# Fused decoder block on one core: output projection split along its contraction, fixed homes for the mixer's tiles, and engine orders from the layer's timeline machine

## The chip, the cores and the metric

The kernel runs as one launch on one core of a Trainium2 chip. A core has five engines that run side by side, each through its own list of instructions in the order in which they stand there: TensorE (PE in the profile, with its weight loads as PEld), VectorE (DVE), ScalarE (ACT), GpSimd (POOL) and SyncE (SP), which here does nothing but issue DMA transfers. The metric is the time of the core in microseconds of device time, lower is better: the median of several runs.

## What is computed

One decoder block over 512 tokens with 2048 channels, in float32. The heart of the reference:

```python
sh1, sc1, gt1, sh2, sc2, gt2 = jnp.split(mod[:, None, :], N_MOD, axis=-1)   # mod = silu(c) @ w_ada + b_ada
h = _rmsnorm(x, norm1_g[l]) * (1.0 + sc1) + sh1
p = h @ w_in[l]
y_rwkv = _rwkv7_mixer(p[..., :N_RWKV_COLS], ...)
y_pool = _pool_mixer(p[..., N_RWKV_COLS:], ...)
mix = jnp.concatenate([y_rwkv, y_pool], axis=-1) @ w_out[l]
x = x + gt1 * mix
h = _rmsnorm(x, norm2_g[l]) * (1.0 + sc2) + sh2
x = x + gt2 * _conv_ffn(h, w_up[l], conv_w[l], conv_b[l], w_down[l])
```

The RWKV mixer has 16 heads of 64 channels, with a state of 64 x 64 per head that is carried from token to token. The pool mixer takes the causal mean over windows of 2, 4, 8 and 16 tokens, for 256 channels each, and multiplies it by a 256 x 256 matrix.

## The kernel before

Everything lies transposed: channels on the 128 partitions, the 512 tokens along them. So x is 16 tiles of 128 x 512. A float32 product is made of three products of the shorter float32r (`mm3`, L115 to L117): the weights are split into a high part `whi` (a copy on ScalarE, L109) and the rest `wlo` (a subtraction on VectorE, L111), the activations likewise (`ah`, `al`). `project` does that for one output tile: it loads weights in pieces of 128 x 512 (`wraw`, ring of 4) and runs 3 products of 128 x 512 for each 128 rows of the contraction. Such a product is called a full-width product below.

The stages in order:

1. The first third of the adaLN product (`ada1`), the first norm, and the first 8 of 35 tiles of the input projection, which are accumulated in all PSUM banks at once.
2. The mixers. The RWKV heads are worked off in four *quads* of four heads (`quad`, g = 0 to 3), two column tiles each. A quad first makes its decays and keys (L376 to L418), then the scores inside chunks of 64 tokens (L427), turns tiles over (L439), inverts 64 x 64 triangular matrices (16 x 16 blocks on VectorE, L478 to L487, then two *levels* of products, L504 to L521), and then goes through the 8 chunks one after the other. This last part is called *the chain* here: for each chunk, state to right-hand side (L538, L540 on VectorE), times the inverse (L544, copied by ScalarE in L545), new state (L554, L557, then L562 on VectorE). After it come the output, its norm and its gate (L571 to L606), and the result is stored to DRAM in `mixd`. All these are small products (64 x 64 and the like), and each step waits for the one before it on another engine.
   Beside the quads run the remaining tiles of the input projection (`win_tile`, 48 full-width products each): the tiles for the next quad in `win_pair` (six for each quad, shifted by a token and stored in DRAM until they are needed), and after the last quad the eight tiles of the pool mixer, each pool group's sums (L274) and products (L289) following its two tiles.
   Beside the quads run also 192 pieces of the adaLN product (`ada_rest`, 48 for each quad): a 128 x 512 piece of weights is loaded (`war`, ring of 3, 256 KB) and multiplied and summed on VectorE (L341).
3. The output projection: 8 output tiles are accumulated at once in blocks of four contraction tiles (`out_block`), then two tiles in full, then the last six in two halves of 256 tokens (`out_half`), so that the second norm of one half runs beside the other.
4. The gated feed-forward part, with the last 64 pieces of the adaLN product in its first group, the second residual and the last norm.

What sets the order: the kernel is written as one sequence with Tile; a scheduler then gives each engine its list. The quads stand under `tc.high_priority(offset=100000)`, so the scheduler takes their instructions first whenever it believes that they can run, and fills in with the rest. The tiles of a quad come from one ring of 12 buffers (`quad_tile`, tag `q4`), in the order of their allocation. All DMA transfers are issued by SP in one list.

Of the kernel before, what the change touches and what calls it, by code (L numbers as in the profile page):

```python
# [46 lines left out]

WIN_ORDER = ["T0", "T1", "T2", "r0", "k0", "v0", "r1", "k1", "v1"]
for _p in range(2, NP):
    WIN_ORDER += [f"r{_p}", f"k{_p}", f"v{_p}"]  # L50
WIN_ORDER += [f"u{_j}" for _j in (6, 7, 2, 3, 4, 5, 0, 1)]


MIX_ORDER = [14, 15, 10, 11, 12, 13, 0, 1, 2, 3, 4, 5, 6, 7, 8, 9]
# [3 lines left out]
def block_kernel(ctx, tc, a, out, stop=None, dbg=None):  # L58
# [16 lines left out]
    scanm = cp.tile([P, 2 * NK, C + 1], F32, tag="scanm", name="scanm")  # L75
    nc.gpsimd.memset(scanm, 1.0)
    nc.gpsimd.memset(scanm[:, :, 0:1], 0.0)
    lanei = cp.tile([P, 16, 16], F32, tag="lanei", name="lanei")
    nc.sync.dma_start(lanei, a["lanei"][:, :, :])
# [25 lines left out]
    def split_weights(src, eng=V):  # L105
        raw = wp.tile([P, WC], F32, tag="wraw", name="wraw", bufs=4)
        nc.sync.dma_start(raw, src)
        hi = wp.tile([P, WC], F32R, tag="whi", name="whi", bufs=3)
        S.copy(hi, raw)  # L109
        lo = wp.tile([P, WC], F32R, tag="wlo", name="wlo", bufs=3)  # L110
        eng.tensor_tensor(lo, raw, hi[:, :].bitcast(F32), op=ALU.subtract)  # L111
        return hi, lo
# [6 lines left out]
    def project(ps, src, acts, start=True, stop=True, engs=(V,)):  # L119

        n = len(acts)
        for k0 in range(0, n, WC // P):
            wh, wl = split_weights(src[:, k0 * P : k0 * P + WC], engs[k0 // 4 % len(engs)])
            for kk in range(WC // P):
# [47 lines left out]
    if True:  # L172
# [53 lines left out]
        if True:  # L226
# [5 lines left out]
            def quad_tile(name):  # L232
                return ra.tile([P, 2 * (16 + T)], F32, tag="q4", name=name, bufs=12)
# [7 lines left out]
            xg = two(quad_tile("xg"))  # L241
# [13 lines left out]
            rkv0 = [quad_tile(n) for n in "rkv"]  # L255
# [4 lines left out]
    def load_pw(gi):  # L260
        t = ra.tile([P, T], F32, tag="war", name="pw", bufs=3)
        pw = t.rearrange("p (i d) -> p i d", i=2)
# [3 lines left out]
    def padded(name):  # L266
        return quad_tile(name).rearrange("p (x t) -> p x t", x=2)

    def pool_front(gi, upad):
        win = WINS[gi]  # L270
        cur, lo, step = upad, 1, 1
        while step < win:
            nxt = padded("sw")
# [4 lines left out]
        z = two(quad_tile("z"))  # L278
        V.scalar_tensor_tensor(z, cur[:, :, 16:], 1.0 / win, upad[:, :, 16:], op0=ALU.mult, op1=ALU.subtract)
        V.tensor_mul(z[:, :, 0:win], cur[:, :, 16 : 16 + win], prec[:, None, 0:win].to_broadcast([P, 2, win]))  # L280
        V.tensor_sub(z[:, :, 0:win], z[:, :, 0:win], upad[:, :, 16 : 16 + win])
        return z

    def pool_back(gi, z, pw):
        ps = batch()
        mx = two(quad_tile("mxp"))
        for d in range(2):
            for i in range(2):
                PE.matmul(ps[:, d, :], pw[:, i, d * P : (d + 1) * P], z[:, i, :], start=i == 0, stop=i == 1)  # L289
            j = gi * 2 + d  # L290
            S.activation(mx[:, d, :], ps[:, d, :], AF.Identity, bias=drv[:, 35 + j : 36 + j], scale=col("psc", j))
            if gi:
                nc.sync.dma_start(mixd[8 + j], mx[:, d, :])
            else:
                last_mix.append(split_act(14 + d, mx[:, d, :]))
# [19 lines left out]
    HEADS = [(x, h) for h in range(2) for x in range(2)]  # L315

# [8 lines left out]
    dx = tc.dram_tile([2, 2, C, 2 * NK, C], F32, name="dx")  # L325
    for w in range(2):
        nc.sync.dma_start(dx[w].rearrange("s i j t -> (s i) (j t)"), sall[:, :, :, :].rearrange("p x c t -> p (x c t)"))

    cq = [None]
    modq = ra.tile([P, 4, 48], F32, tag="modq", name="modq")  # L330

    def ada_rest(n0, n1):
        for n in range(n0, n1):
            kq, j = divmod(n, 48)
            if j == 0:
                cq[0] = ra.tile([P, T], F32, tag="cq", name="cq")
                nc.sync.dma_start(cq[0], cact[0:1, kq * T : (kq + 1) * T].partition_broadcast(P))
            wa = ra.tile([P, T], F32, tag="war", name="war", bufs=3)
            nc.sync.dma_start(wa, a["ada2"][kq, j, :, :])
            jk = ra.tile([P, T], BF16, tag="jkr", name="jkr")  # L340
            V.scalar_tensor_tensor(jk, wa, 1.0, cq[0], op0=ALU.mult, op1=ALU.mult,  # L341
# [20 lines left out]
    def quad(g, rkv):  # L362
# [15 lines left out]
        sg = quad_tile("sg")  # L378
        V.memset(lead(sg)[:, :, 0:1], 0.0)
# [3 lines left out]
        al = quad_tile("al")  # L383
        for x in range(2):
            S.activation(two(al)[:, x, :], psal[:, x, :], AF.Sigmoid, bias=c2("a0", x))
        cs = quad_tile("cs")
        n = 2 * NK * (C + 1)
        V.tensor_tensor_scan(cs[:, 0:n], scanm[:, :, :].rearrange("p c t -> p (c t)"), sg[:, 0:n], 0.0,
                             op0=ALU.mult, op1=ALU.add)
        mid = ra.tile([P, 2 * NK, 1], F32, tag="mid", name="mid")  # L390
        V.tensor_copy(mid, lead(cs)[:, :, C // 2 : C // 2 + 1])
        V.tensor_sub(lead(cs), lead(cs), mid[:, :, :].to_broadcast([P, 2 * NK, C + 1]))
        ep = quad_tile("ep")
        S.activation(ep[:, 0:n], cs[:, 0:n], AF.Exp, scale=-Q)
        em = quad_tile("em")
        S.activation(em[:, 0:n], cs[:, 0:n], AF.Exp, scale=Q)
        fdec = ra.tile([P, 2 * NK - 1, 1], F32, tag="fdec", name="fdec")
# [588 lines left out]
```

## Time and profile before

| | |
|---|---|
| median of 3 runs | 2460.82 us (2457.5 to 2462.72) |
| the profiled execution, its own time | 2459.58 us |
| its span from the first to the last instruction | 2457.8 us |
| TensorE busy | 2254.7 us (92%), 14178 instructions |
| VectorE busy | 1345.9 us (55%) |
| ScalarE busy | 831.7 us (34%) |
| moved by DMA | 352.98 MB, 144 GB/s on average |
| granted TensorE clock, mean | 0.970 |

How to read it: the span is cut into stages by what TensorE does in them. In the part from 1400 us to 2400 us TensorE has work in every microsecond; there, only fewer or shorter products could change the time. Before 722 us it waits in many places, and there the time hangs on which waits end last. "Idle before, releaser" in a row of the trace is how long the engine stood still before that instruction and what ended it. PEclk is the share of full clock that TensorE was granted.

### The profile page before, as it was taken

The numbers are of one execution on the slowest core, as the hardware profiler recorded it, in microseconds if no ns is written. First come the engines' busy times: TensorE is split into PE (matmuls) and PEld (weight loads), VectorE is DVE, ScalarE is ACT, GpSimd is POOL, SyncE is SP. The second block draws the span as 40 slices with busy tenths as digits, with TensorE's granted clock in tenths as the row PEclk, the third lists the DMA queues.
The fourth block names the chain that finished last, engine by engine and source line by source line (L and its number), as shares of the span: only waits on it lengthen the run. The fifth ranks groups of instructions, "written<-read, shape, count | busy, mean of one in ns | idle before, by whom it ended". The sixth has DMA issues, their size and how long they took to land.

```text
span 2457.8 us, 36667 instructions
## 1 busy us (share of the span) xinstructions
PE 2254.7 (92%) x14178; PEld 1829.3 (74%) x14178; DVE 1345.9 (55%) x2398; ACT 831.7 (34%) x1351; POOL 23.5 (1%) x26
## 2 busy tenths in 40 slices
PE   4878888888379999999999999999999999999997
PEld 3656566565257889987888888888888888888887
DVE  7987686766434457757634443444344434444457
ACT  3243252523233335532223322333233322323333
POOL 0000000000000001100000000000000000000000
PEclk9989899999679999999999999999999999999998
DMA  9965757656103635538532233333323332332335
GB/s 357 340 221 163 240 176 222 213 177 208 40 32 120 198 111 181 190 105 260 170 98 98 95 98 96 99 96 97 97 97 99 95 99 95 98 97 97 99 97 174
DMA packets 204418, 352.98 MB, mean 144 GB/s; under 512 B 46033, under 2 KB 52049, under 8 KB 200017
## 3 DMA queue, kind: packets, MB, share of 16 engines
q1 hardware_dynamic: 204242, 350.63, 44.7%
q8 instruction: 111, 1.82, 0.3%
q14 instruction: 65, 0.53, 0.1%
HBM read 335.33 MB, written 15.21 MB: 143 GB/s over the span
## 4 chain that ended last, share of the span: by engine, by line
PE 63%; DMA 2%; DVE 2%; ACT 0%; issue 0%; POOL 0%; DVEq 0%; SPq 0%; ACTq 0%; POOLq 0%
PE b L115 20%; PE b L117 19%; PE b L116 19%; DMA slot<-ada 1%; DMA wraw<-wup 1%; PE bt L115 1%; PE bt L117 1%; PE bt L116 1%; DVE slot L810 1%; PE mm L115 0%; PE mm L117 0%; PE mm L116 0%; DVE wlo L111 0%; PE bt L289 0%; DVE x L863 0%
## 5 line engine op out<-in xcount | busy, mean ns | idle before, releaser
L111 DVE TENSOR_TENSOR wlo<-wraw,whi 128x512 fp32r<-128x512 f32 x772 | 532.3, 692 | 714.9 <-ACT whi L109 700.4
L109 ACT CAST whi<-wraw 128x512 fp32r<-128x512 f32 x788 | 488.5, 622 | 1240.7 <-PE b L116 931.2
L117 PE MATMUL b<-hh,wlo 128*128 128x512 f32 (+1 forms) x1472 | 560.6, 381 | 7.1 <-DVE wlo L111 6.8
L115 PE MATMUL b<-hh,whi 128*128 128x512 f32 (+1 forms) x1472 | 559.9, 380 | 0.0
L116 PE MATMUL b<-hl,whi 128*128 128x512 f32 (+1 forms) x1472 | 559.5, 380 | 0.0
L115 PE MATMUL b<-ah,whi 128*128 128x512 f32 (+1 forms) x992 | 353.3, 357 | 1.9 <-ACT whi L109 1.9
L117 PE MATMUL b<-ah,wlo 128*128 128x512 f32 (+1 forms) x992 | 352.1, 355 | 0.8 <-DVE wlo L111 0.8
L116 PE MATMUL b<-al,whi 128*128 128x512 f32 (+1 forms) x992 | 352.2, 355 | 0.0
L117 PEld LDWEIGHTS b<-hh,wlo 128*128 128x128 f32 x1472 | 277.0, 188 | 62.8 <-DVE wlo L111 9.5
L116 PEld LDWEIGHTS b<-hl,whi 128*128 128x128 f32 x1472 | 277.0, 188 | 52.5
L115 PEld LDWEIGHTS b<-hh,whi 128*128 128x128 f32 x1472 | 277.0, 188 | 52.4 <-ACT whi L109 0.6
L115 PEld LDWEIGHTS b<-ah,whi 128*128 128x128 f32 x992 | 187.7, 189 | 30.9 <-ACT ah L136 2.3
L117 PEld LDWEIGHTS b<-ah,wlo 128*128 128x128 f32 x992 | 187.7, 189 | 27.3 <-DVE wlo L111 1.2
L116 PEld LDWEIGHTS b<-al,whi 128*128 128x128 f32 x992 | 187.7, 189 | 27.2 <-DVE al L137 1.2
L117 PE MATMUL mm<-ah,wlo 128*128 128x512 f32 x464 | 190.4, 410 | 14.7 <-DVE wlo L111 14.7
L115 PE MATMUL mm<-ah,whi 128*128 128x512 f32 x464 | 189.3, 408 | 8.7 <-ACT whi L109 8.7
L116 PE MATMUL mm<-al,whi 128*128 128x512 f32 x464 | 187.7, 404 | 0.0
L341 DVE SCALAR_TENSOR_TENSOR jkr<-war,cq 128x512 bf16<-128x512 f32 x192 | 132.1, 688 | 60.9 <-DMA war<-ada 50.5
L117 PEld LDWEIGHTS mm<-ah,wlo 128*128 128x128 f32 x464 | 88.4, 191 | 43.8 <-DVE wlo L111 22.3
L848 DVE SCALAR_TENSOR_TENSOR x<-b,mod,x 128x512 f32<-128x512 f32 x80 | 59.7, 750 | 110.9 <-PE b L117 110.8
L115 PEld LDWEIGHTS mm<-ah,whi 128*128 128x128 f32 x464 | 88.7, 191 | 32.5 <-ACT whi L109 9.1
L116 PEld LDWEIGHTS mm<-al,whi 128*128 128x128 f32 x464 | 88.5, 191 | 21.7 <-issue 3.5
(267 smaller groups left out, 1926.4 us busy)
## 6 DMA issues: line engine op xcount, KB each, us to landing
wraw<-wup SPq DMA_DIRECT2D x368, 256.0 KB
war<-ada SPq DMA_DIRECT2D x192, 256.0 KB
wraw<-wdn SPq DMA_DIRECT2D x192, 256.0 KB
wraw<-win SPq DMA_DIRECT2D x140, 256.0 KB
wa<-ada SPq DMA_DIRECT2D x32, 1024.0 KB
wraw<-wout SPq DMA_DIRECT2D x88, 256.0 KB
slot<-ada SPq DMA_DIRECT2D x64, 256.0 KB
sp<-spill SPq DMA_DIRECT2D x18, 256.0 KB
```

Source lines behind the costliest of these rows:

```text
L109: S.copy(hi, raw)
L111: eng.tensor_tensor(lo, raw, hi[:, :].bitcast(F32), op=ALU.subtract)
L115: PE.matmul(ps, wh, xh, start=start, stop=False)
L116: PE.matmul(ps, wh, xl, start=False, stop=False)
L117: return PE.matmul(ps, wl, xh, start=False, stop=stop)
L341: V.scalar_tensor_tensor(jk, wa, 1.0, cq[0], op0=ALU.mult, op1=ALU.mult, accum_out=modq[:, kq, j : j + 1])
L810: V.scalar_tensor_tensor(jk, wa, 1.0, cbs[kq], op0=ALU.mult, op1=ALU.mult, accum_out=modg[:, kq, j : j + 1])
L848: V.scalar_tensor_tensor(x2[f], ps, mod[:, 80 + f : 81 + f], x2[f], op0=ALU.mult, op1=ALU.add)
```

## The change

- **Order.** `TileContext(nc, schedule_with_timeline_sim=True)`: the engines' lists now come from the layer's timeline machine.
- **Input projection.** The tiles of the pool groups are made before the tiles of the last quad, in the iteration g = 2; they are stored to DRAM (`su`) and loaded again by `pool`. The four pool groups stand behind the third quad, under high priority, and their results go to `mixd` all four.
- **Output projection.** The contraction is ordered as pool tiles, then quads 0 to 3. For the first `NW` = 10 output tiles the first `NM` = 14 of 16 contraction tiles are done while the last quad runs: product, times the gate, plus x, stored as `part` in DRAM. The last quad's result is split at once into `M[14:16]` and never goes to DRAM. Afterwards `part` comes back as x2 and only the two last contraction tiles are added. The tiles 10 to 15 are done in halves as before.
- **adaLN product.** The same 96 x 2048 numbers are cut into 96 pieces of 128 x 1024 (512 KB), 24 for each quad; the ring `war` has 2 buffers, which the pool matrices `pw` share; the product is written over its input instead of to a bfloat16 tile.
- **Quads.** `quad` is split into `front` and `rest`. Each tile has a home of its own (`cell(tag)`: R, K, V, X, Y, EM, EP, AL, INV, TB, TK, TV, PM) instead of a place in a ring. The inverse's transpose Y is made by TensorE and ScalarE from X (L536, L539) instead of through DRAM; X is cleared by GpSimd and only its diagonal blocks are loaded (8 transfers after one store, for 24 stores and 2 loads). One preloaded table set serves Ln and Exp. In the chain, the two products of the new state change places.

The core of the diff:

```diff
-MIX_ORDER = [14, 15, 10, 11, 12, 13, 0, 1, 2, 3, 4, 5, 6, 7, 8, 9]
+MIX_ORDER = [8 + 2 * _g + _i for _g in POOLS for _i in range(2)] + [0, 1, 2, 3, 4, 5, 6, 7]
+NM = 14
...
     def load_pw(gi):
-        t = ra.tile([P, T], F32, tag="war", name="pw", bufs=3)
+        t = ra.tile([P, 2 * T], F32, tag="war", name="pw", bufs=2)
...
-            wa = ra.tile([P, T], F32, tag="war", name="war", bufs=3)
+            wa = ra.tile([P, 2 * T], F32, tag="war", name="war", bufs=2)
             nc.sync.dma_start(wa, a["ada2"][kq, j, :, :])
-            jk = ra.tile([P, T], BF16, tag="jkr", name="jkr")
-            V.scalar_tensor_tensor(jk, wa, 1.0, cq[0], op0=ALU.mult, op1=ALU.mult,
+            V.scalar_tensor_tensor(wa, wa, 1.0, cq[0], op0=ALU.mult, op1=ALU.mult,
                                    accum_out=modq[:, kq, j : j + 1])
...
+        with tc.issue_after(act.ins):
+            act = S.preload_act_table_set("natural_log_exp_and_others")
...
+        dxy = tc.dram_tile([P, 16, 16], F32, name=f"dxy{g}")
+        nc.sync.dma_start(dxy, xyl[:, 0, :, :])
         for s in range(2):
             for i in range(4):
                 o = 64 * s + 16 * i
-                e = slice(16 * i, 16 * i + 16)
-                nc.sync.dma_start(dx[0, s, e, :, e].rearrange("a j t -> j a t"), xyl[o : o + 16, 0, :, :])
-                nc.sync.dma_start(dx[1, 1 - s, e, 0:NK, e].rearrange("a j t -> j a t"), xyl[o : o + 8, 1, :, :])
-                nc.sync.dma_start(dx[1, s, e, NK:, e].rearrange("a j t -> j a t"), xyl[o + 8 : o + 16, 1, :, :])
-        X, Y = quad_tile("X"), quad_tile("Y")
-        for w, t in enumerate((X, Y)):
-            nc.sync.dma_start(flat(t), dx[w].rearrange("s i j t -> (s i) (j t)"))
+                nc.sync.dma_start(rows(X)[o : o + 16, :, 16 * i : 16 * i + 16],
+                                  dxy[o : o + 16].rearrange("j a t -> a j t"))
...
     for g in range(NQ):
-        if g + 1 < NQ:
-            win_pair(2 * g + 2)
-            win_pair(2 * g + 3)
+        if g < NQ - 1:
+            if g == 2:
+                for n, gi in enumerate(POOLS):
+                    for i in range(2):
+                        ps = win_tile(21 + 2 * n + i)
+                        t = ra.tile([P, T], F32, tag="spill", name="spill", bufs=2)
+                        S.copy(t, ps)
+                        d = tc.dram_tile([P, T], F32, name=f"su{gi}_{i}")
+                        nc.sync.dma_start(d, t)
+                        su[gi, i] = d
+            at = (9, 15, 29)[g]
+            win_pair(2 * g + 2, at)
+            win_pair(2 * g + 3, at + 3)
...
+        with hp():
+            rest(g, rkv, fr)
+            if g == 2:
+                for gi in POOLS:
+                    edge = pool(gi)
+        ada_rest(24 * g, 24 * g + 24)
...
+    for i in range(NM):
         load_mix(i)
...
+    for f in range(NW):
+        if f % 2 == 0:
+            xt = two(cell("K" if f % 4 == 0 else "R", "xt"))
+            nc.sync.dma_start(xt, a["xT"][:, f : f + 2, :])
+        ps = mmtile()
+        project(ps, a["wout"][f, :, 0 : NM * P], M)
+        V.scalar_tensor_tensor(xt[:, f % 2, :], ps, mod[:, 32 + f : 33 + f], xt[:, f % 2, :], op0=ALU.mult, op1=ALU.add)
+        d = tc.dram_tile([P, T], F32, name=f"part{f}")
+        nc.sync.dma_start(d, xt[:, f % 2, :])
+        part.append(d)
+    M += last_mix
...
-    with tile.TileContext(nc) as tc:
+    with tile.TileContext(nc, schedule_with_timeline_sim=True) as tc:
```

What the new order looks like is seen in two places. The first is TensorE in the third quad (g = 2), at the two levels of its inverse. Names: `mm` is a PSUM tile of a full-width product, `bt` one of a quad's, `ch` that of the chain. Before:

```order
L513 MATMUL bt<-pm,Y 64x64 x32
L519 MATMUL bt<-Y,pm 64x64 x32
L504 MATMUL bt<-X,sb 64x64 x32
L115 MATMUL mm<-ah_1004,whi 128x512
L116 MATMUL mm<-al_1005,whi 128x512
L117 MATMUL mm<-ah_1004,wlo 128x512
L115 MATMUL mm<-ah_224,whi 128x512
L116 MATMUL mm<-al_225,whi 128x512
L117 MATMUL mm<-ah_224,wlo 128x512
L115 MATMUL mm<-ah_276,whi 128x512
L116 MATMUL mm<-al_277,whi 128x512
L519 MATMUL bt<-Y,pm 64x64 x32
```

The same place now:

```order
L536 MATMUL bt<-cmat,X 64x64 x32
L546 MATMUL bt<-X,sb 64x64 x32
L298 MATMUL mm<-z,pw 128x512 x4
L555 MATMUL bt<-pm,Y 64x64 x32
L561 MATMUL bt<-Y,pm 64x64 x32
L546 MATMUL bt<-X,sb 64x64 x32
L298 MATMUL mm<-z,pw 128x512 x4
L561 MATMUL bt<-Y,pm 64x64 x32
L570 MATMUL bt<-tokTV,sk 64x64 x32
L613 MATMUL bt<-ar,sall 64x64 x4
L298 MATMUL mm<-z,pw 128x512 x4
L586 MATMUL ch<-xv,Y 64x64 x4
```

The tiles of the input projection that stood between the third quad's steps have moved forward: all 1296 of their products stand ahead of the third quad's own first products, 692 from the first quad's first product to the second quad's, and 604 from there to the third's. In the chains of these two quads about 20 full-width products stand between one step and the next, where 2 to 4 stood before. Beside the third quad only the 16 pool products (L298, four groups of four) are left; the next full-width product of a projection stands behind the last quad's L411.

The second place is VectorE in the same quad's chain. `sall` is the state, `R` (now `rc`) the right-hand side, `war` an adaLN piece, `mxl` a mixer tile loaded from `mixd` whose low part `al` is made. Before:

```order
L562 SCALAR_TENSOR_TENSOR sall<-ch,fdec,sf 128x64 x2
L341 SCALAR_TENSOR_TENSOR jkr,modq<-war,cq 128x512
L540 TENSOR_TENSOR R<-ch,xv 128x128
L341 SCALAR_TENSOR_TENSOR jkr,modq<-war,cq 128x512 x2
L562 SCALAR_TENSOR_TENSOR sall<-ch,fdec,sf 128x64 x2
L111 TENSOR_TENSOR wlo<-wraw,whi 128x512
L341 SCALAR_TENSOR_TENSOR jkr,modq<-war,cq 128x512
L540 TENSOR_TENSOR R<-ch,xv 128x128
```

And now:

```order
L606 TENSOR_SCALAR sall<-ch,fdec 128x64 x2
L344 SCALAR_TENSOR_TENSOR war,modq<-war,cq 128x1024
L141 TENSOR_TENSOR al_6993<-mxl,ah_6992 128x512
L582 TENSOR_TENSOR rc<-ch,xv 128x128
L344 SCALAR_TENSOR_TENSOR war,modq<-war,cq 128x1024
L141 TENSOR_TENSOR al_6999<-mxl,ah_6998 128x512
L604 SCALAR_TENSOR_TENSOR sall<-ch,fdec,sf 128x64 x2
L344 SCALAR_TENSOR_TENSOR war,modq<-war,cq 128x1024
L582 TENSOR_TENSOR rc<-ch,xv 128x128
L344 SCALAR_TENSOR_TENSOR war,modq<-war,cq 128x1024
L141 TENSOR_TENSOR al_7005<-mxl,ah_7004 128x512
L604 SCALAR_TENSOR_TENSOR sall<-ch,fdec,sf 128x64 x2
```

The adaLN pieces are twice as wide and stand in two groups. 48 of the 96 stand in the first quad up to the end of its levels, none in the second; the other 48 stand behind the third quad's first chain step (26 up to its mixer product L648, 22 from there to the last quad's level mask L549). Between the groups the two buffers of the ring hold the matrices of the first two pool groups.

More of the change, by code (lines that the diff above doesn't have):

```diff
@@ L315, in block_kernel @@
     HEADS = [(x, h) for h in range(2) for x in range(2)]
+    TURNS = [(x, h) for x in range(2) for h in range(2)]
     def tk(x, h):
@@ L324, in block_kernel @@
     G.memset(sall, 0.0)
[L325 to L327 removed]
     cq = [None]
[L330 removed]
+    modq = ra.tile([P, 2, 48], F32, tag="modq", name="modq")
     def ada_rest(n0, n1):
@@ L360, in cells, with front @@
         return ps[:, :, :].rearrange("p x (c t) -> p x c t", t=C)
-    def quad(g, rkv):
+    def front(g, rkv):
         r, k, v = rkv
@@ L411, in quad, with rest, c2 @@
                                    op0=ALU.mult, op1=ALU.mult)
+        return lws, al, ep, em, inv, fdec
+    def rest(g, rkv, fr):
+        r, k, v = rkv
+        lws, al, ep, em, inv, fdec = fr
+        def c2(name, x):
+            return col(name, 2 * g + x)
         ar = ra.tile([P, 2 * NK, 2, C], F32, tag="ar", name="ar")
@@ L465, in quad @@
                                    op0=ALU.mult, op1=ALU.mult)
-        tb = by_token(bt, ident)
-        tkk = by_token(kt, ident)
-        tv = by_token(v, cent)
-        sk = scores("k")
+        tb = by_token("TB", bt, ident)
+        ktx = ktv.rearrange("p (x c) t -> p x c t", x=2)[:, :, :, 1:]
+        ps = batch()
+        for c in range(NK):
+            for x, h in HEADS:
+                PE.matmul(cells(ps)[tk(x, h), x, c, :], ktx[HS[h], x, c, :], ident[HS[h], HS[h]], start=True, stop=True)
+        tkk = cell("TK", "tokTK")
+        S.copy(flat(tkk), wide(ps))
+        tkk = slab(tkk)
+        tv = by_token("TV", v, cent)
+        sk = ra.tile([P, 2, NK, 2, C], F32, tag="sk", name="sk")
+        for hh in range(2):
+            ps = batch()
+            for c in range(4):
+                for x, h in HEADS:
+                    PE.matmul(ps[tk(x, h), x, 128 * c : 128 * c + 128], ktx[HS[h], x, 4 * hh + c, :],
+                              arx[HS[h], x, 4 * hh + c, :, :], start=True, stop=True)
+            V.tensor_tensor(sk[:, :, 4 * hh : 4 * hh + 4, :, :].rearrange("p x c w t -> p x c (w t)"),
+                            ps[:, :, :].rearrange("p x (c u) -> p x c u", c=4),
+                            masks[:, :, :].rearrange("p w t -> p (w t)")[:, None, None, :].to_broadcast(
+                                [P, 2, 4, 2 * C]), op=ALU.mult)
         psb = batch()
@@ L624, in block_kernel @@
     shift(win_tile(8), 17, two(rkv0[2])[:, 1, :])
-    rkv = rkv0
+    edge = []
     for g in range(NQ):
-        if g + 1 < NQ:
-            win_pair(2 * g + 2)
-            win_pair(2 * g + 3)
-        with hp():
+        if g < NQ - 1:
+            if g == 2:
+                for n, gi in enumerate(POOLS):
+                    for i in range(2):
+                        ps = win_tile(21 + 2 * n + i)
[7 more added lines that the diff above has]
+            win_pair(2 * g + 3, at + 3)
+        with hp(), ExitStack() as after:
+            for i in edge:
+                after.enter_context(tc.issue_after(i.ins))
+            rkv = rkv0
@@ L664, in load_mix @@
         M.append(split_act(i, t))
-    def out_block(f, k0):
-        return project(pss[f], a["wout"][f, :, k0 * P : (k0 + 4) * P], M[k0 : k0 + 4], start=k0 == 0, stop=k0 == KT - 4)
-    zs = pool_front(0, upad)
-    for i in range(4):
+    for i in range(NM):
         load_mix(i)
-    banks = [batch(), chain()]
-    pss = [t[:, i, :] for t in banks for i in range(2)]
-    for f in range(4):
-        last = out_block(f, 0)
-    with tc.issue_after(last.ins):
-        pool_back(0, zs, pw)
-    bank2 = batch()
-    pss += [mmtile(), mmtile(), bank2[:, 0, :], bank2[:, 1, :]]
-    for f in range(4, 8):
-        out_block(f, 0)
+    part = []
+    for f in range(NW):
+        if f % 2 == 0:
+            xt = two(cell("K" if f % 4 == 0 else "R", "xt"))
+            nc.sync.dma_start(xt, a["xT"][:, f : f + 2, :])
+        ps = mmtile()
+        project(ps, a["wout"][f, :, 0 : NM * P], M)
[4 more added lines that the diff above has]
+    M += last_mix
     psctx.close()
```

229 lines of the change are left out of this document (113 added, 116 removed).

## Prediction, made before the changed kernel ran

> **What bounds the kernel now.** I read the page's slices first (40 of 61 us each), then cut the span by windows at the stages, then counted the full-width products of the input projection (PSUM tile `mm`) in them.
>
> ```profile
> PE   4878888888379999999999999999999999999997
> DVE  7987686766434457757634443444344434444457
> PEclk9989899999679999999999999999999999999998
> ```
>
> TensorE is short of full up to slice 12; from 13 on it is full, so nothing but a shorter way to there, or fewer products behind, moves the end. The windows, as start and length, then busy time of PE, PEld, DVE, ACT, POOL, then granted clock, DMA share and GB/s:
>
> ```profile
> 163.00:266.00 103.00, 87.44 (x962) 67.34 (x964) 74.54 (x166) 31.03 (x43) 0.00 (x0) 0.91 0.60 189
> 266.00:313.00 47.00, 41.82 (x547) 26.07 (x540) 30.43 (x88) 19.27 (x38) 0.00 (x0) 0.95 0.72 223
> 313.00:460.00 147.00, 125.78 (x1496) 92.37 (x1494) 104.12 (x248) 51.98 (x85) 0.00 (x0) 0.95 0.67 206
> 460.00:605.00 145.00, 123.50 (x1488) 89.07 (x1487) 100.07 (x240) 49.60 (x81) 0.00 (x0) 0.98 0.66 205
> 605.00:616.40 11.40, 10.15 (x40) 5.29 (x40) 7.88 (x10) 8.83 (x14) 0.00 (x0) 1.00 0.26 86
> 616.40:686.00 69.60, 27.67 (x714) 22.50 (x716) 31.13 (x55) 14.49 (x16) 0.00 (x0) 0.63 0.12 28
> 686.00:722.00 36.00, 24.14 (x440) 17.34 (x441) 10.34 (x27) 13.06 (x29) 0.00 (x0) 0.67 0.01 2
> 722.00:911.70 189.70, 188.88 (x798) 148.91 (x797) 82.99 (x123) 65.80 (x107) 0.00 (x0) 1.00 0.43 141
> 1400.00:2400.00 1000.00, 1000.00 (x4440) 827.63 (x4439) 437.41 (x633) 311.86 (x500) 0.00 (x0) 1.00 0.32 97
> ```
>
> Three quads (163 to 605) are covered by products; the last (605 to 722, 117 us) runs bare: from 616.4 on PE is busy 27.67 of 69.6 us at clock 0.63. Then comes a dense stretch with the pool tiles and the output projection. The last row gives the pitch of dense full-width products: 1000 / 4440 = 0.225 us. Of tile `mm` alone:
>
> ```profile
> 163.00:605.00 442.00, 262.33 (x988) 182.33 (x988) 14.12 (x19) 12.98 (x19) 0.95 0.65 204
> 163.00:266.00 103.00, 61.45 (x249) 46.76 (x249) 3.73 (x5) 3.41 (x5) 0.91 0.60 189
> ```
>
> 988 products cost 988 x 0.225 = 222 us of the 442, so each covered quad costs 147 us, 73 of them for itself. That is what cover brings: 73 where a bare quad costs 117.
>
> **The change part by part.** The sum runs from 163 to the place where output tiles are done in halves, which both kernels pass; before it is at 911.71 (second row), and behind it little moves:
>
> ```profile
> 911.49 0.39 PE L117 MATMUL b<-ah,wlo 128*128 128x512 f32 x1
> 911.71 0.28 PE L115 MATMUL b<-ah,whi 128*128 128x256 f32 x1
> ```
>
> The first stage, to 163, keeps its order. Where I count instructions between two steps, the count is that of the engines' new lists.
>
> *First quad, up to the end of its levels (103 us before).* VectorE gets 48 wide adaLN pieces in place of 42 narrow ones. Its rows before, and the loads' issues at SP in a stretch where nothing else hinders them:
>
> ```profile
> L341 DVE SCALAR_TENSOR_TENSOR jkr<-war,cq 128x512 bf16<-128x512 f32 x42 | 28.9, 688 | 12.6 <-DMA war<-ada 12.0
> L341 DVE DVE_READ_ACCUMULATOR jkr<-war,cq 128x1 f32 x42 | 3.4, 82 | 0.0
> L414 DVE SCALAR_TENSOR_TENSOR ar<-inv,ep 128x1024 f32<-128x1024 f32 x1 | 1.2, 1217 | 0.0
> 564.75 7.00 SPq L339 DMA_DIRECT2D war<-ada  x6
> ```
>
> A wide piece should take 1.22 + 0.08 = 1.30 us (the row of L414, plus the accumulator); 46 of them lie here: 60 us. VectorE: 74.5 - 32.3 + 60 = 102 us. It was idle for 103 - 74.5 = 28.5, 12 of that already waiting for these loads. Loads came at 7.00 / 6 = 1.17 us for 256 KB, an estimated 2.33 for 512 KB: 46 x 2.33 = 107, near VectorE's 102. Waits for TensorE's replies remain, so 102 + 25 = 127; ends: 103 (all fits in the old idle time) and 137 (102 plus 28.5 and a few more). It ends at 290.
>
> *First quad's chain and tail.* 470 products stand here: 105.8 us, and about 19 for the quad's own products: 125, ending at 415. Nothing else can bind: about 20 products (4.5 us) between steps cover each.
>
> *Second quad.* Up to its levels no adaLN piece and 149 products: a bare quad's 605 to 686 (81) less 6, below: 75 to 77, in whose idle time the products fit; 492. Chain and tail: 433 x 0.225 = 97.4 + 20 = 117; 609. So both quads together end about where the third ended before, with 308 more products done.
>
> *Third quad, bare now, with the pools.* I start from 117. Off: two table loads and the way of X and Y:
>
> ```profile
> 621.46 1.28 ACT L407 ACT_TABLE_LOAD   x1
> 627.03 1.28 ACT L408 ACT_TABLE_LOAD   x1
> 658.53 0.27 SPq L493 DMA_DIRECT2D dx<-xyl  x1
> 667.99 0.34 SPq L497 DMA_DIRECT2D X<-dx  x1
> 671.25 1.99 PE L504 MATMUL bt<-X,sb 64*64 64x64 f32 x64 [22.62 <-DMA X<-dx]
> ```
>
> 24 stores and two loads took 658.53 to 671.25 = 12.7 us. Now one store and the loads of the blocks take two landings of 3.3 (667.99 to 671.25) and some 1.5 for eight issues, 8.1: 4.6 less, if the new transposes on TensorE and ScalarE lie under the later blocks. Of the two table loads I take one as on the path. Together -6.
>
> On: the pool groups. Their sums stand on VectorE ahead of the level masks (first row; 1.25 us each, second row):
>
> ```profile
> 673.29 1.23 DVE L507 TENSOR_TENSOR pm<-bt,mlev 128x1024 f32<-128x1024 f32 x1 [14.37 <-PE bt L504]
> 716.54 1.25 DVE L274 TENSOR_TENSOR sw<-sw 128x1050 f32<-128x1050 f32 x1
> ```
>
> 10 sums and 4 products of 1.2 us, with small ones and splits, are about 21 us; the idle stretch ahead of L507 (14.37) takes 9 to 14: +10 (0 to 15). In the chain and tail 26 wide pieces wait at one per 2.33 us of load: 60.6, where the stretch 686 to 722 has 36: +25; ends +13 (VectorE alone: 10.3 + 26 x 1.30 + mixer splits) and +35 (steps queued behind them). Behind the tail the result goes through DRAM, and the last quad's cover must wait for it:
>
> ```profile
> 644.99 0.44 SPq L451 DMA_DIRECT2D dn<-sb  x1
> 648.47 0.34 SPq L453 DMA_DIRECT2D nl<-dn  x1
> 650.49 0.42 DVE L478 TENSOR_TENSOR xyl<-nl,lanei 128x256 f32<-128x256 f32 x1 [2.78 <-DMA nl<-dn]
> ```
>
> A store and load took 5.5 us (644.99 to 650.49); with stores queued ahead, the split and the first weights I take 10 (5 to 15); it lies beside the start of the last quad only in part. Sum: 117 - 6 + 10 + 25 + 10 = 156 (130 to 175); 765.
>
> *Last quad, covered.* Its own first steps need nothing of the round trip and start beside it, at 755. To its mask a bare quad takes 673.29 - 605 = 68, less 6; 190 products (43 us of TensorE) and 22 wide pieces (22 x 2.33 = 51 us of loads) stand there too, whose splits and sums VectorE must fit in between. I take half of the products' time as not hidden: +23, so 85, to 840. The levels took 13 (673.29 to 686) and have products between them now: 20, to 860. Five chain steps hold 230 products: 51.8 + 5. Three steps are bare, and the tail. What those cost, with the tail's store:
>
> ```profile
> 687.36 0.34 PE L554 MATMUL ch<-ua,tok 64*64 64x64 f32 x8 [0.39 <-ACT ua L545]
> 690.08 0.34 PE L554 MATMUL ch<-ua,tok 64*64 64x64 f32 x8 [0.39 <-ACT ua L545]
> 693.18 0.49 PE L554 MATMUL ch<-ua,tok 64*64 64x64 f32 x8 [0.38 <-ACT ua L545]
> 696.54 0.49 PE L554 MATMUL ch<-ua,tok 64*64 64x64 f32 x8 [0.39 <-ACT ua L545]
> 730.26 0.80 SPq L608 DMA_DIRECT2D mixd<-rs  x2
> ```
>
> A step took 2.72 us at first (687.36 to 690.08) and 3.36 later (693.18 to 696.54): 3 x 3.36 = 10. Eight steps from 686 end near 711, and the result is stored at 730.26: a tail of 20. So 755 + 85 + 20 + 57 + 10 + 20 = 947, which is 182 behind 765 (ends 160, if pieces and splits fit in the old idle time, and 195). The `part` tiles' loads and sums hide beside it, at most +2.
>
> The steps slow down with the clock (0.63 and 0.67 in the bare windows). The Trainium skill, page "TensorE: Matmul & The Clock Gate", section "Part 1: The HAM clock gate (the "warmup" mystery)", has the clock fall to half after an idle window of about 3.4 us and come back after one of work. The trace agrees in kind (the third step is the first slow one); by that rule the first bare step would still be warm, 0.6 us less here, and the pools' products, now in the bare third quad, would run at half rate, an estimated 2 to 7 us more. I don't count it.
>
> *Meeting point.* 60 products, 13.5 us, remain of the first ten output tiles: 947 + 13.5 = 960.5, against 911.7. The dense stretch (190 us) has gone, but its products didn't fit for nothing. The rest, from there to the end, has the same products: 0, to +2. So the profiled time of 2459.6, 1.2 below the median, becomes 2459.6 + 49 + 1 = **2510**.
>
> **The rivals.**
>
> *Faster: the wide pieces don't bind.* If loads of two buffers overlap as those of three did, and VectorE's idle time takes the pieces, the first stretch stays at 103, the second quad's at 70, the third quad costs 131 (117 - 6 + 10 pools + 10 round trip) and the last 160. The sum: 163 + 103 + 125 + 70 + 117 + 131 + 160 + 13.5 = 882.5, 29 less: 2430. For it: the covered quads already hide 48 narrow pieces, and no window before is above 75% on VectorE. Against: 12 us of L341's idle time was waiting for loads already, and half of all pieces now lie in that one stretch, where 42 of 192 lay. The two sums are 78 us apart; the sign turns where less than 29 of these show.
>
> *No change.* Half of the added cost shows: say 110, 72, 143, 170 in those four places: 913.5, +2: about 2462.
>
> *Slower still: one load at a time.* In the third quad's chain SP's list has `mixd` stores and loads between the piece loads, and an issue that waits for its tile blocks those behind it. If each wide load is then served alone, 3.3 us of landing + 0.4, the 48 late pieces cost 178 us instead of the 48 x 2.33 = 112 that I took; about 55 of that shows: 2565.
>
> **How the numbers follow.** My sum 0.68 (own range 2475 to 2545, from the ends of the four stretches; their ends don't all meet); the faster rival 0.16; no change 0.07; slower still 0.09. What a measurement can tell from no change here is about 0.2%, 5 us. Faster by more: 0.16; within: 0.06; slower by more: 0.78. From 2445 to 2555 it leaves out most of the faster rival and the slowest.
>
> **What would show it.** In the new profile: first chain step of the first quad near 290 (103 us after 163 speaks for the faster rival); VectorE idle before L344 released by its loads; the second quad's first products near 415; PEclk near 0.65 in a stretch of some 150 us from 610; first output products near 765 and covered steps to 920; first half-wide product near 960. I am wrong if the third quad takes under 135 us, or the last under 160.

## The result and the profile after

The changed kernel takes **2539.52 us** (median of 4 runs, 2537.56 to 2541.31), the kernel before 2459.16 beside it: a ratio of 1.0331, 95% interval [1.0305, 1.0357], slower. I had forecast 2510 and slower; the loss is 80 us where I had 50. The profiled execution has a span of 2539.5 us.

The page's slices of the changed kernel, in the same columns as those of before:

```profile
PE   4876699898446697999999999999999999999997
DVE  7986534523667535775844443444334443444457
PEclk9988799999667898999999999999999999999998
```

TensorE is full from slice 17 on, where it was from slice 13 (a slice is 63 us now). The hole of slices 11 and 12 has grown into slices 11 to 14, with the low clock (0.6, 0.6, 0.7) inside it. Ahead of the half-wide tiles I cut the span where the prediction cut it: first quad up to its levels, its chain and tail, the second quad in the same two parts, the third quad up to the first output product, the last quad up to the first of the 60 last full-width products, these 60; and the whole. Columns as in the windows of before:

```profile
155.60:302.00 146.40, 95.46 (x1036) 72.00 (x1036) 103.09 (x176) 31.56 (x45) 0.95 (x1) 0.81 0.71 216
302.00:424.00 122.00, 121.95 (x882) 94.75 (x882) 39.12 (x70) 39.76 (x74) 0.95 (x1) 0.98 0.34 111
424.00:502.40 78.40, 67.00 (x970) 50.59 (x969) 44.76 (x75) 27.06 (x39) 0.00 (x0) 0.93 0.35 99
502.40:618.20 115.80, 115.80 (x867) 89.93 (x867) 33.11 (x62) 35.43 (x68) 0.95 (x1) 1.00 0.28 89
618.20:802.00 183.80, 88.19 (x1285) 51.71 (x1284) 118.42 (x202) 54.86 (x84) 0.95 (x1) 0.66 0.52 163
802.00:979.50 177.50, 144.40 (x1631) 111.39 (x1632) 90.13 (x171) 43.12 (x80) 0.00 (x0) 0.88 0.45 139
979.50:999.90 20.40, 17.17 (x60) 13.47 (x59) 13.10 (x25) 8.81 (x17) 0.00 (x0) 0.81 0.77 264
155.60:999.90 844.30, 649.96 (x6721) 483.84 (x6722) 441.73 (x779) 240.61 (x403) 3.81 (x4) 0.86 0.47 146
```

The same stretch took 748.7 us before (163 to 911.7). Before the stretch the kernel is 7.4 us ahead (155.6 for 163.0), behind it another 6.5 (1539.6 for 1546.1), so 95.6 - 13.9 = 82 are lost. The places to look at are the first and the fifth row, where TensorE stands still for 51 and 96 us. In rows two and four, where the first two quads go through their chains, it never stands still.

What VectorE waits for in the first row, and then from the third quad's chain to the first output product, by its groups of the wide pieces (columns as before):

```profile
L344 DVE SCALAR_TENSOR_TENSOR war<-war,cq 128x1024 f32<-128x1024 f32 x46 | 56.3, 1223 | 37.4 <-DMA war<-ada 37.1
...
L344 DVE SCALAR_TENSOR_TENSOR war<-war,cq 128x1024 f32<-128x1024 f32 x30 | 36.7, 1224 | 31.1 <-DMA war<-ada 31.0
```

And the chain of waits in the third quad's chain, from 730 to 753 us (start, length, what):

```profile
730.39 4.14 DMA war<-ada
...
734.72 1.06 issue
735.78 0.08 DVE war L344
735.86 0.03 DVE sall L604
735.89 4.35 DMA war<-ada
...
740.34 1.24 DVE war L344 x2
741.60 4.44 DMA war<-ada
...
746.14 1.23 DVE war L344 x2
747.38 0.03 DVE rc L582
747.40 4.22 DMA war<-ada
...
752.87 0.08 DVE war L344
752.95 0.03 DVE sall L604
```

Read it as a column of loads: each takes 4.1 to 4.4 us, a sum follows, and the next load on the chain begins when its buffer comes free. Now and then one of the quad's own steps (`sall`, `rc`) gets its 0.03 us on the chain. They don't wait for TensorE; they stand behind a piece in VectorE's list. From its first state product on TensorE (709.37) to its last right-hand side on VectorE (758.39) this chain takes 49 us, where the last quad's bare chain before took 21 (687.36 to 708.79).

### The profile page after: what moved, and what is told of

Its sections match the earlier page's. It is cut to its first block, busy times and chain, and to the rows that moved or that the text cites. A ratio compares the mean times of both kernels' runs of the same rounds, so it can differ in the third digit from the quotient of the medians.

```text
span 2539.5 us, 36907 instructions
## 1 busy us (share of the span) xinstructions
PE 2271.9 (89%) x14434; PEld 1840.8 (72%) x14434; DVE 1345.7 (53%) x2230; ACT 818.2 (32%) x1349; POOL 27.6 (1%) x30
## 4 chain that ended last, share of the span: by engine, by line
PE 75%; DMA 10%; DVE 9%; issue 3%; ACT 1%; SPq 1%; POOL 0%; DVEq 0%; ACTq 0%; POOLq 0%
PE b L120 19%; PE b L118 19%; PE b L119 19%; DMA war<-ada 5%; PE mm L118 4%; PE mm L120 4%; PE mm L119 4%; DVE war L344 2%; DMA slot<-ada 1%; DVE wlo L114 1%; PE pf L118 1%; SPq L466 1%; DVE jk L211 1%; PE pf L119 1%; DVE slot L851 0%
## 5 line engine op out<-in xcount | busy, mean ns | idle before, releaser
L114 DVE TENSOR_TENSOR wlo<-wraw,whi 128x512 fp32r<-128x512 f32 (+1 forms) x782 | 532.2, 683 | 756.6 <-ACT whi L112 743.0
L112 ACT CAST whi<-wraw 128x512 fp32r<-128x512 f32 (+1 forms) x798 | 490.1, 616 | 1305.6 <-PE b L119 926.2
L120 PE MATMUL b<-hh,wlo 128*128 128x512 f32 (+1 forms) x1472 | 546.7, 380 | 0.5 <-DVE wlo L114 0.5
L120 PE MATMUL mm<-ah,wlo 128*128 128x512 f32 x572 | 232.1, 406 | 5.8 <-DVE wlo L114 5.7
L118 PE MATMUL mm<-ah,whi 128*128 128x512 f32 x572 | 232.1, 406 | 5.6 <-ACT whi L112 5.6
L119 PE MATMUL mm<-al,whi 128*128 128x512 f32 x572 | 230.5, 403 | 0.0
L344 DVE SCALAR_TENSOR_TENSOR war<-war,cq 128x1024 f32<-128x1024 f32 x96 | 117.4, 1223 | 80.1 <-DMA war<-ada 79.7
L120 PEld LDWEIGHTS mm<-ah,wlo 128*128 128x128 f32 x572 | 110.1, 193 | 35.2 <-DVE wlo L114 9.1
L118 PEld LDWEIGHTS mm<-ah,whi 128*128 128x128 f32 x572 | 110.1, 192 | 34.8 <-ACT whi L112 7.0
L119 PEld LDWEIGHTS mm<-al,whi 128*128 128x128 f32 x572 | 110.5, 193 | 24.4 <-issue 1.3
```

The costliest lines, as they stand in the source:

```text
L112: S.copy(hi[:, 0:w], raw[:, 0:w])
L114: eng.tensor_tensor(lo[:, 0:w], raw[:, 0:w], hi[:, 0:w].bitcast(F32), op=ALU.subtract)
L118: PE.matmul(ps, wh, xh, start=start, stop=False)
L119: PE.matmul(ps, wh, xl, start=False, stop=False)
L120: return PE.matmul(ps, wl, xh, start=False, stop=stop)
L344: V.scalar_tensor_tensor(wa, wa, 1.0, cq[0], op0=ALU.mult, op1=ALU.mult, accum_out=modq[:, kq, j : j + 1])
```

## The experiments

The kernels ran in three groups of four, in the order of their numbers, each group on one chip beside the kernel before, whose median was 2454.42, 2455.53 and 2455.44 us. All differences to the changed kernel are to its 2539.52. Two theories stood against each other. **P**: the wide adaLN pieces bind. **F**: the order that the timeline machine makes costs, whatever the pieces are.

### The pieces left out (e1_noada)

```diff
     modq = ra.tile([P, 2, 48], F32, tag="modq", name="modq")
+    G.memset(modq, 0.0)
...
-        ada_rest(24 * g, 24 * g + 24)
```

> The changed kernel with the 96 wide adaLN pieces of the mixers left out (their loads and sums, with the numbers set to zero), so that part of the computation is not done. Theory P (the pieces bind: two buffers, each taken by a load of 4.3 us and a sum of 1.25 us, one piece per 2.8 us, on the chain of waits in the first quad's front, the third quad's chain and the last quad's front): about 110 us less, 2430, with the first quad's first chain step 60 us earlier, the third quad's tail 20 earlier and the last quad's front 30 shorter. Theory F (the order of the timeline machine costs, whatever the pieces are: 60 products between chain steps of the first two quads, nothing beside the third): at most 40 us less, 2500 or more, since the order of the products stays.

Measured: 2427.55 us, 112 less. Theory P had this number. The second quad's first product came at 351.8 in place of 424, the last quad's at 681.3 in place of 777. One thing in the expectation was not so: the order of the products did not stay. The machine makes its lists anew for each program, and in this one 608 of the input projection's products stand in the first quad where the changed kernel has 692, and 67 beside the third where it has none. So the 112 us are what the pieces cost together with the order that comes with them.

### Narrow pieces, four buffers (e2_narrow4)

```diff
-            wa = ra.tile([P, 2 * T], F32, tag="war", name="war", bufs=2)
-            nc.sync.dma_start(wa, a["ada2"][kq, j, :, :])
-            V.scalar_tensor_tensor(wa, wa, 1.0, cq[0], op0=ALU.mult, op1=ALU.mult,
-                                   accum_out=modq[:, kq, j : j + 1])
+            for q in range(2):
+                wa = ra.tile([P, T], F32, tag="war", name="war", bufs=4)
+                nc.sync.dma_start(wa, a["ada2"][2 * kq + q, j, :, :])
+                V.scalar_tensor_tensor(wa, wa, 1.0, cq[0][:, q * T : q * T + T], op0=ALU.mult, op1=ALU.mult,
+                                       accum_out=modq[:, 2 * kq + q, j : j + 1])
```

The pool matrices' ring, the sums over the pieces and the packing of the weights follow.

> The changed kernel with each wide piece cut into two of 128x512 and a ring of four of half the size in the same space (the pool matrices take from it as before). Theory P: four loads are under way in place of two, a pair of narrow pieces takes some 2.0 us in place of 2.8, half of that shows on 96 pieces: 40 us less, 2500. Theory F: within 10 us of the changed kernel's 2540.

Measured: 2537.73 us, no gain. Theory P's mechanism, the ring of two, fails here. Windows of this kernel for the third quad and the last one, and the group of its narrow pieces from 717 to 800 us:

```profile
610.50:789.70 179.20, 78.61 (x1262) 49.94 (x1262) 120.17 (x282) 42.08 (x68) 0.95 (x1) 0.66 0.56 175
789.70:1000.40 210.70, 170.75 (x1712) 125.27 (x1713) 108.25 (x214) 64.81 (x113) 0.00 (x0) 0.88 0.42 134
```

```profile
L345 DVE SCALAR_TENSOR_TENSOR war<-war,cq 128x512 f32<-128x512 f32 x70 | 47.1, 689 | 19.6 <-DMA war<-ada 19.1
```

The waits for loads are shorter: 19.6 us for 70 narrow pieces, where 30 wide ones had 31.1. But the machine made a new order out of it and put more of the pieces into the third quad (78 narrow ones, as much as 39 wide ones, where 23 wide ones stood), which now takes 179.2 us from its first product to the last quad's (158.8 with wide pieces); the first quad gained 8 and the last 12. Shorter waits did not help here, since more of the pieces were put on the path. What four buffers would bring in an unchanged order, this run does not tell.

### The flag taken back (e3_oldsched)

```diff
-    with tile.TileContext(nc, schedule_with_timeline_sim=True) as tc:
+    with tile.TileContext(nc) as tc:
```

> The changed kernel with its one flag taken back (TileContext(nc), no timeline machine); the program is the same. All four quads then have products beside them (3 to 8 between chain steps), and 498 stand between the third quad and the last. Theory F: four covered quads at 73 us of their own and 1776 products at 0.225 us make 692 us where the kernel before has 749: about 55 less than before, 2405. Theory P: the wide pieces are on the path in this order too, 96 at 2.8 us where 192 narrow ones were hidden: 2480 or more.

Measured: 2431.13 us, ratio to the kernel before 0.9907 [0.9887, 0.9927]. The whole loss comes from this one word: 108 us. The rest of the change is a gain of 23. Theory F is right in sign and too high in size: it had 55, from 692 us between the first quad and the half-wide tiles, and the stretch took 717 (162.3 to 879.4). A step of the chain is counted here from one new state to the next. The rhythm of the second quad's chain in this kernel and, below it, of the first quad's chain in the changed one, by VectorE's timeline:

```profile
400.42 0.48 DVE L604 SCALAR_TENSOR_TENSOR sall<-ch,fdec,sf 128x64 f32<-128x64 f32 x2 [1.21 <-PE ch L599]
403.71 0.48 DVE L604 SCALAR_TENSOR_TENSOR sall<-ch,fdec,sf 128x64 f32<-128x64 f32 x2 [1.81 <-PE ch L599]
```

```profile
346.89 0.48 DVE L604 SCALAR_TENSOR_TENSOR sall<-ch,fdec,sf 128x64 f32<-128x64 f32 x2 [1.75 <-PE ch L599]
362.24 0.48 DVE L604 SCALAR_TENSOR_TENSOR sall<-ch,fdec,sf 128x64 f32<-128x64 f32 x2 [1.75 <-PE ch L599]
```

With 7 products in it a step takes 3.29 us, no more than a bare one (3.36). With 60 it takes 15.35. Those some 50 further products, 12 us, fill no gap there, and they are missing where there are gaps. Why 7 products cost nothing is seen in the granted clock, first in that covered chain, then in the bare chain of the kernel before:

```profile
396.00:411.00 15.00, 14.74 (x225) 8.84 (x227) 5.44 (x17) 5.34 (x16) 0.00 (x0) 1.00 0.19 66
690.68:707.50 16.82, 10.76 (x212) 8.13 (x212) 3.89 (x16) 4.26 (x15) 0.00 (x0) 0.50 0.01 2
```

The bare chain runs at 0.50 although TensorE is busy for 10.76 of 16.82 us; the covered one at 1.00. At the full clock a bare step takes 2.70 to 2.72 us. So the 7 products lengthen a step by some 0.6 us, which is what the lower clock adds to a bare one.

### The flag alone, on the kernel before (e4_before_tl)

```diff
-    with tile.TileContext(nc) as tc:
+    with tile.TileContext(nc, schedule_with_timeline_sim=True) as tc:
```

> The kernel before with the flag alone added (schedule_with_timeline_sim=True), its program unchanged. Its lists put some 60 products between the chain steps of the first quad, 313 in the second, none beside the third and the last quad, and 384 behind. Theory F: 232 + 135 + 117 + 117 + 207 = 808 us from the first small products to the half-wide tiles where before has 749: about 60 more than before, 2520. Theory P: the pieces stay narrow with three buffers, so no loss: within 15 us of 2460.

Measured: 2561.68 us, 107 more than before. The flag costs the same in both programs. My 60 were too low; the windows of its four quads say where:

```profile
156.70:473.00 316.30, 240.46 (x1902) 180.65 (x1902) 214.98 (x543) 74.82 (x124) 0.00 (x0) 0.86 0.74 235
473.00:608.00 135.00, 110.40 (x1435) 83.57 (x1436) 60.88 (x111) 46.80 (x75) 0.00 (x0) 0.87 0.27 85
608.00:719.30 111.30, 56.56 (x1164) 38.34 (x1164) 44.45 (x85) 32.92 (x51) 0.00 (x0) 0.65 0.14 38
719.30:831.00 111.70, 57.36 (x1163) 38.80 (x1164) 47.52 (x88) 31.97 (x51) 0.00 (x0) 0.62 0.08 22
```

The second is as I had it (135), the third and the last take 111 for my 117, and what follows up to the half-wide tiles 191 for my 207. The first takes 316 for my 232: 190 of the 192 pieces, narrow and in a ring of three, stand in it, and VectorE waits for their loads:

```profile
L341 DVE SCALAR_TENSOR_TENSOR jkr<-war,cq 128x512 bf16<-128x512 f32 x190 | 131.2, 690 | 77.4 <-DMA war<-ada 65.9 <-DMA cq<-cact 5.1 <-issue 4.4
```

A step of its chain with 63 products and 13 pieces takes 22.1 us (384.02 to 406.11), where one with 60 products and no piece takes 15.35. So neither the width nor the ring of two is needed for the pieces to bind; it is enough that they stand together in one quad. This is read from the trace: the pieces were not left out of this kernel.

### The pieces left out with the old order (e5_oldsched_noada, e6_before_noada)

The edits are those of the first and the third experiment, and in the kernel before the same lines (`ada_rest(48 * g, 48 * g + 48)`).

> The changed kernel without its flag and without the 96 wide adaLN pieces of the mixers (that part of the computation is not done). Theory Q (the pieces cost where the machine's order puts them, ahead of the quads' steps on VectorE, and nothing where they fill idle time): within 15 us of the 2431 with them. Rival R (the pieces cost wherever they stand, by their bytes and VectorE's time): as much as with the flag, about 110 less, 2320.

> The kernel before without the 192 narrow adaLN pieces of its mixers (that part of the computation is not done). Theory Q: they were hidden, within 15 us of 2454. Rival R: 80 or more less, 2375.

Measured: 2371.74 (59 less than with them) and 2391.14 us (64 less). Both theories miss: the pieces are not hidden in the old order, and they don't cost 110 either. So of the 112 us of the first experiment some 60 are paid in the old order too, by both programs, and 50 more in the machine's. That gives the change's 80 in parts: the program -23; the machine's order +56 without the pieces (2427.55 against 2371.74); the pieces' place in it +52 (together 85, since the kernel before ran some 4 us faster in these groups than beside the changed kernel). The parts are differences between whole kernels, each with lists of its own, and not stretches of one.

The 56 show in TensorE's busy time, for the same 6720 instructions from the first quad to the half-wide tiles, first with the machine's order and no pieces, then with the old order and no pieces:

```profile
155.90:886.30 730.40, 625.98 (x6720) 469.30 (x6721) 335.28 (x587) 240.18 (x404) 3.82 (x4) 0.91 0.32 101
```

```profile
161.30:819.20 657.90, 604.85 (x6720) 451.57 (x6721) 331.05 (x588) 238.59 (x403) 2.87 (x3) 0.97 0.36 112
```

It stands still for 104 us in the first and 53 in the second, and works 21 longer at the lower mean clock (0.91 for 0.97): 72 us together, of which the kernel with the machine's order has 13 back outside the stretch (5.4 ahead of it, 7.6 behind).

### The pieces moved to the chains (e7_adachain)

```diff
-        ada_rest(24 * g, 24 * g + 24)
+        if g < 2:
+            with tc.issue_after(mark.ins):
+                ada_rest(48 * g, 48 * g + 48)
```

`mark` is the chain's first new state on VectorE.

> The changed kernel, flag and ring as they are, with all 96 wide pieces made to stand behind the first step of the chain on VectorE, 48 in the first quad and 48 in the second, where VectorE was idle for 85 of 130 us. Theory Q: nearly all that leaving the pieces out brought, about 2440. Rival R: the same bytes and sums through the same two buffers at 2.8 us, 2 x 48 x 2.8 = 269 us where two chains give 260: little gain, 2520 or more.

Measured: 2490.05 us, 49.5 less. It lies between the two expectations, and it is 62.5 above the kernel without pieces: so the time of the excess of 52 is gone, and the 60 that the old order pays remain. Where the pieces stand costs, and it is about those 50 us. The rest is paid in the chains now: a step of the first quad's chain with 63 products takes 18.5 us (262.34 to 280.83), where it took 15.35 with 60 and no piece.

### The tiles held back (e8_hold), the two together (e10_hold_adachain), and without pieces (e11_noada_hold)

```diff
+            cover = ExitStack()
+            if g:
+                cover.enter_context(tc.issue_after(last.ins))
...
             win_pair(2 * g + 3, at + 3)
+            cover.close()
```

`last` is the last state product of the quad before.

> The changed kernel with the input projection's tiles of each iteration held behind the last chain step of the quad before, so that 580 of their products stand beside the third quad in place of none, and fewer beside the first two. The pieces stay where they are in the first quad. If the bare third quad costs as I priced it (159 us where a covered one has 73 of its own), the time falls by 25 to 40, about 2505. If a quad costs the same wherever its cover stands, since TensorE's products only move, within 10 us of 2540.

> The changed kernel with its flag, with both edits: input tiles held behind the quad before, and the wide pieces behind the first chain steps of the first two quads. If the placement of the pieces (52 us) and the missing cover beside the third quad (the rest of the flag's 108 us) are separate costs, most of both comes back: about 2450. If holding the tiles brings only the 15 us that it brought alone: 2475.

> The changed kernel with its flag, without the adaLN pieces (that part of the computation is not done), and with the input tiles held behind the quad before. It asks what the flag's order of the products costs when no piece is in the way: 2428 with the flag's own order, 2372 with the old one. If the bare third quad is what costs, about 2385. If the clumps of 60 products between chain steps cost, which stay, 2415 or more.

Measured: 2524.24, 2499.07 and 2417.21 us. Holding the tiles gave 15 us with the pieces as they were, nothing with the pieces in the chains (9 more than without), and 10 with no pieces. So covering the third quad brings back a fifth of the 56 us; as the edit takes that cover from the first two quads, it does not say what the missing cover costs as a whole. Once the tiles are held, the third quad's chain steps have 60 to 63 products each. Without pieces the first quad's products are used up after three steps and the second's after one, with bare ones behind. The hole moved, its size stayed: without pieces TensorE stands still for 104 us as before, by this kernel's window over the same stretch:

```profile
155.70:880.70 725.00, 621.50 (x6720) 468.68 (x6721) 333.38 (x585) 240.23 (x404) 3.82 (x4) 0.91 0.33 101
```

725.0 less 621.5 is 103.5. That the clumps are what costs fits this, and fits the chains' 15.35 and 3.29 us; it was not tried with an order of the machine that has no clumps, so it is argued, not shown. The flag also makes the lists of the other engines anew, and no run here keeps those apart from TensorE's.

### The old order with the old ring (e9_old_n3_pw)

The edit of the second experiment on the kernel without the flag, with `bufs=3`, and the pool matrices in a ring of their own (`tag="pw"`).

> The changed kernel without its flag, and the adaLN pieces as the kernel before has them: 128x512, a ring of three, with a ring of its own for the pool matrices (so pieces may stand beside the second and third quad too, where the shared ring kept them out). If the pieces cost about 60 us wherever they stand (as in both kernels with the old order), within 10 us of 2431. If their clumping into the first and last quad costs in this order too, 20 less: 2410.

Measured: 2434.13 us, ratio 0.991 [0.989, 0.9929], the same as with wide pieces and the shared ring. In the old order neither the form nor the ring of the pieces makes a difference that shows. The kernel without the flag stays the best of all that compute everything, 1% faster than before.

### One part alone: X and Y (e12_before_xy)

In the kernel before, the 24 stores and two loads give way to the changed kernel's one store, eight loads, transposes (TensorE) and copy (ScalarE).

> The kernel before with one part of the change alone: X's diagonal blocks by one store and eight loads, X cleared by GpSimd, and Y made from X by TensorE and ScalarE. My sum had 4.6 us for the bare quad. If the three covered quads gain nothing, 2 to 5 us less than before; if each of the four waits for it, 15 to 20 less; if the old way was hidden in all, no change.

Measured: 2450.37 us, ratio 0.9978 [0.9963, 0.9992], 5 us less. The rows of the bare quad are the inverse's first step on VectorE, the level's first products on TensorE and its mask on VectorE:

```profile
643.53 0.42 DVE L478 TENSOR_TENSOR xyl<-nl,lanei 128x256 f32<-128x256 f32 x1 [2.30 <-DMA nl<-dn]
```

```profile
657.57 0.42 PE L509 MATMUL bt<-X,sb 64*64 64x64 f32 x2
```

```profile
662.83 1.23 DVE L512 TENSOR_TENSOR pm<-bt,mlev 128x1024 f32<-128x1024 f32 x1 [10.84 <-PE bt L509]
```

The first two products come 14.0 us after the step, where the first came after 20.8 before (650.49 to 671.25). But the other 62 of the level stand behind the transposes on TensorE, and the mask needs them all. It comes after 19.3 us, for 22.8 before (650.49 to 673.29): 3.5 less, for my 4.6. Up to the chain's first new state it is 4.8 less (32.7 for 37.5), with a granted clock of 0.82 from 657 to 674 us, where the levels before had 0.69 (671 to 686). That is about the gain that was measured (2 to 9 us by the interval), so a gain in the covered quads is not shown.

## Why the prediction was right, and where its sum was short

The sign and the way were right: the sum followed the lists stretch by stretch, and most of its stretches came out. The first quad's chain and tail: 125, measured 122. The second quad: 77 and 117, measured 78 and 116. The last quad from its first output product: 182, measured 178. X and Y: right in kind, a little large (4.6 for 3.5 up to the mask). The clock in the bare stretch: 0.66, as expected. Of the three bare steps at the end the first took 2.70 us and the next 3.34:

```profile
954.12 0.48 DVE L604 SCALAR_TENSOR_TENSOR sall<-ch,fdec,sf 128x64 f32<-128x64 f32 x2 [1.39 <-PE ch L599]
956.82 0.47 DVE L604 SCALAR_TENSOR_TENSOR sall<-ch,fdec,sf 128x64 f32<-128x64 f32 x2 [1.38 <-PE ch L599]
960.16 0.47 DVE L604 SCALAR_TENSOR_TENSOR sall<-ch,fdec,sf 128x64 f32<-128x64 f32 x2 [1.78 <-PE ch L599]
```

The granted clock around them, with the same columns as the windows above:

```profile
951.40:956.80 5.40, 2.66 (x81) 1.83 (x80) 2.05 (x6) 1.39 (x5) 0.00 (x0) 0.98 0.29 97
956.80:962.00 5.20, 4.06 (x114) 3.69 (x118) 1.53 (x6) 1.34 (x4) 0.00 (x0) 0.50 0.01 3
```

So the clock went down with a delay, which I had not counted (0.6 us). The Trainium skill, page "TensorE: Matmul & The Clock Gate", section "Part 1: The HAM clock gate (the "warmup" mystery)", has the half clock come after an idle window of about 3.4 us. The trace agrees in kind: the last full-width product began at 951.02, and the clock held for some 5 us after it, in which TensorE was busy half of the time.

Two stretches were outside their bounds, both mainly by the same term, **the pace of a wide piece**. I took 2.33 us, from six narrow loads in a row. Up to the first quad's levels: 127 forecast (103 to 137), 146.4 measured. VectorE's own work came as I had it, 103.1 us for 102. But I had let the loads run beside it and put all its waiting, 25 us, down to TensorE's replies; it waited 43.3 us, 37.4 of them ahead of a piece. From the third quad's first product to the first output product: 156 forecast (130 to 175), 183.8 measured. Up to the chain's first state product it took 91 us for my 85, the chain and its tail 81 (709.4 to 790.1) for my 61, the way through DRAM 12 for my 10. The 26 pieces of the chain and tail took 3.1 us each, not 2.33: 26 x 0.77 = 20 of the 28. The row of these loads on the page, with KB each and the median us from issue to landing:

```profile
war<-ada SPq DMA_DIRECT2D x96, 512.0 KB, 4.3
```

A load takes 4.3 us and not the 3.3 of a lone one, so I estimate that two buffers give at best (4.3 + 1.3) / 2 = 2.8; that the quad's own steps between the pieces make the rest is argued, not shown. These two stretches are 19 and 28 us over the sum. The 60 last products took 20.4 for 13.5, at a clock of 0.81, and the other rows together 7 less than forecast: 47 over the stretch. Ahead of it and behind it the kernel was 14 us shorter where I had 1 longer. So 50 + 47 - 15 = 82: what I had missed outside the stretch, where I took the first stage's order as unchanged, made up for part of what I had missed inside it, and that part is luck. The rival with one load at a time (3.7 us) was a little nearer in this term than my sum.

One reason was wrong, though my sum does not rest on it. For the faster rival I wrote that the covered quads already hide 48 narrow pieces, and the expectations behind it went on from there. They were not hidden: they cost 64 us, and by the trace 60 to 67 of them stand in each of the three covered quads and none in the last. The changed kernel pays some 50 more, and it is not the width that makes it (with narrow pieces and four buffers the time is the same) but that the machine's order packs them ahead of a quad's steps.

And a question that I did not ask is the answer to most of it. I summed an order as given and did not separate who made it. The program of the change is faster by 23 us under the old scheduler, which is near the rival "faster" (2430 forecast for pieces that don't bind, 2431 measured without the flag); but the way was another than I gave there, so that number was met by luck; the flag costs 108 in the one program and 107 in the other.

## What to carry to other kernels

A change that has both a new program and a new order is two changes: build the one without the other before pricing either, here one word. Cover is worth what the gap takes: 7 products in a step of a latency-bound chain (one whose steps wait for each other) were free, the next 50 cost their full time and were missing elsewhere. Fillers on an engine whose list is in order should be priced by leaving them out: "hidden" pieces cost some 60 us in the old order, and nearly twice that in an order that put them together ahead of the steps of a chain.

## What the runs showed of the hardware

The first stage ended at 155.0 to 157.0 us in the profiled runs of all eight kernels with the flag, and at 161.3 to 163.4 in the six without it. From the first half-wide product to the end it was 1537.4 to 1540.4 us with the flag and 1546.0 to 1547.9 without. So the machine's order is good for some 6 us in the first stage, which loads most of the time (DMA share 0.89), and for 6 to 9 behind the mixers; why was not followed up. The 108 and 107 us of the flag are a balance: in the profiled runs it loses 127 and 116 us in the stretch between, and gains 13 and 15 outside it.
